# Modulation products of a two-layer diffusion step: from the mixers to VectorE in the feed-forwards

## The chip, the core and the metric

One core of a Trainium2 chip runs the whole program. It has a matrix engine (TensorE, PE in the profile), a vector engine (VectorE, DVE), an activation engine (ScalarE, ACT), GpSimd (POOL) and SyncE (SP), which issues the loads here. Each engine takes its instructions in a fixed order. The metric is the device time of one execution, in microseconds.

## What is computed

One step of a diffusion backbone: two layers with their own weights, 384 tokens (128 context, 256 latent) of width 1024, everything in float32. Cut to what matters here, a layer is

```python
mod = silu(cond) @ w_mod[l] + b_mod[l]        # nine vectors m[0..8] of 1024, for two conditions
h = x * (1 + m[1]) + m[0]
x = layer_norm(ALPHA * x + 0.5 * m[2] * swiglu(h, w_ffn_up[0], w_ffn_down[0]))
h = x * (1 + m[4]) + m[3]
x = layer_norm(ALPHA * x + m[5] * mixer(h))   # attention and a gated scan side by side
h = x * (1 + m[7]) + m[6]
x = layer_norm(ALPHA * x + 0.5 * m[8] * swiglu(h, w_ffn_up[1], w_ffn_down[1]))
```

The vectors hang on the conditions alone, `c` for latent and `c_ctx` for context tokens. So they can be worked out at any time before their use. There are eighteen, written (layer, number) below; one reads 4 MB of `w_mod`.

## The kernel before

**Stages.** The program runs feed-forward (0,0), mixer 0, feed-forward (0,1), then the same three for layer 1. Between two of them lies a boundary: a LayerNorm over the whole width, after which the next input can be made. I call the boundaries b0 to b4, and the feed-forwards the first to the fourth. In the profiled execution the first feed-forward lies at 31 to 319 us, mixer 0 at 329 to 521, the second feed-forward at 530 to 815, the third at 825 to 1102, mixer 1 at 1113 to 1306 and the fourth to 1595.

**Products.** Activations are transposed, 128 channels by 384 tokens to a chunk. A weight tile of 1 MB (`ws`, three buffers, L293) is cut in pieces; ScalarE rounds a piece to `wh` (L313), VectorE subtracts it from the original into `wl` (L314), and TensorE does three matmuls for each chunk (`mm3`, L318 to L320): high by high, high by low (`hl`), low by high. In a feed-forward's up half (22 columns f of two products each) VectorE also multiplies gate and value (L481) and makes the low part of the result (L483). In the down half it adds the product to the residual X (L349); there are 12 weight tiles, three to a pair of output chunks.

**Modulation.** The class `Pump` holds all modulation work as a list of groups, cut into steps that are taken in the list's order. Each step takes one 1 MB tile of `w_mod` (`wm`, three buffers, loaded by SP at L189). A group has one of two forms:
- the tensor form (`add_tensor`, L236): the tile goes through TensorE with the silu of the conditions as stationary operand, in four strips of 32 columns, with one or two vectors side by side. One vector takes four steps; a pair takes eight.
- the vector form (`add_vector`): half a vector, in two steps. VectorE multiplies each 128 x 512 piece by the conditions' values for the partitions and adds it up in `gsum` (L248 for the first, L250 for the others), for both conditions: 2 multiplications and 14 multiply-adds. The closing sum over the partitions (`finish`) is 8 small matmuls of `gsum` against `rows`, again at L236.

In both forms `finish` ends with a transposition (`gmt`, L228) and an addition (L229) on VectorE.

**Where steps are taken.** `PUMPED` says which vectors have which form, and in what order. `PLAN` gives, for each feed-forward, the columns of its up half and the tiles of its down half at which a step is taken; `NEXT_STEPS` the steps at each boundary (`next_input`); `MIX_STEPS` those in a mixer before its output product. So before, twelve half vectors run on VectorE beside the up halves of the first two feed-forwards, and (0,5) to (0,8), (1,0), (1,2) and (1,5) to (1,8) go through TensorE at boundaries and in the mixers.

**Order.** A scheduler orders each engine's instructions by priority as they become possible; `tc.high_priority` pulls the weight splits (by PIECE_AHEAD) and the normalisation (by CHAIN_AHEAD) ahead. Steps that are written behind a mixer's attention are therefore partly pulled forward into its products.

Of the kernel before, what the change touches and what calls it, by code (L numbers as in the profile page):

```python
# [14 lines left out]
PSUM = bass.MemoryType.PSUM  # L15

P = 128
D = 1024
KD = D // P
# [35 lines left out]
def by_vector(*mods):  # L55
    """Groups of modulation products taken by the vector engine: one vector's half each."""
    return [([x], c, c + HALF, True) for x in mods for c in (0, HALF)]


def by_tensor(*mods):  # L60
    """A group of modulation products taken by the tensor engine."""
    return [(list(mods), 0, KD, False)]


PUMPED = (by_vector((0, 2), (0, 3), (0, 4)) + by_tensor((0, 5)) + by_tensor((0, 6), (0, 7)) + by_tensor((0, 8), (1, 0))
          + by_vector((1, 1), (1, 3), (1, 4)) + by_tensor((1, 2)) + by_tensor((1, 5), (1, 6)) + by_tensor((1, 7), (1, 8)))
UP = [f for f in range(3, 21) if f % 3]
PLAN = ((UP, ()), (UP, ()), ((), ()), ((), ()))
NEXT_STEPS = (3, 3, 4, 3, 3)
MIX_STEPS = (14, 10)  # L70
# [3 lines left out]
def hybrid_step_kernel(ctx: ExitStack, tc: tile.TileContext, A):  # L74
# [91 lines left out]
    class Pump:  # L166
        """The modulation products, cut into steps that other work takes in where it suits it.

        A group has some (layer, vector) pairs and a range of their 128-wide chunks; a step takes as many
        of the contraction's chunks as fill a tile."""  # L170
# [68 lines left out]
        def add_vector(self, gi, wv, k0):  # L239
            """Sums each partition's own rows, for the ones of add_tensor to sum over the partitions."""  # L240
# [63 lines left out]
    def piece(src):  # L304
        """Exact float32 weights [P, a, b] as two float32r parts, the second what the first leaves."""
# [22 lines left out]
    def rstd_columns(ps, n, eps, name):  # L328
        """n token tiles of mean squares in ps[:, :n] -> their reciprocal roots."""
# [6 lines left out]
    class Residual:  # L336
        """Post-norm of alpha*x + gate*y, with y coming in chunk by chunk."""
# [38 lines left out]
        def moments(self):  # L376
            """Token-major mean (in PSUM) and reciprocal deviation; the mean also along the partitions."""
# [24 lines left out]
    class LastResidual(Residual):  # L402
        """Turned to token-major rows as it comes in, for the result."""
# [590 lines left out]
```

## Time and profile before

| | us |
|---|---|
| three runs | 1617.20, 1614.57, 1615.80 |
| median | 1615.8 |
| profiled execution, first to last instruction (span) | 1610.9 |
| TensorE matmuls busy | 1554.1 |
| TensorE weight loads busy | 1445.0 |
| VectorE busy | 948.3 |
| ScalarE busy | 659.3 |
| GpSimd busy | 163.0 |

The runs are of whole executions; the page doesn't give the profiled execution's own time beside its span, and the median lies 4.9 us above the span. Of the chain of waits that ends last 86% is TensorE, 5% VectorE and 2% DMA. A stretch of the trace is read by its busy columns: an engine that fills it in matmuls and in weight loads has nothing to spare, one that fills it in matmuls alone may still wait, since matmuls overlap. The granted clock is in parts of 2.4 GHz.

### The profile page before, as it was taken

To read this page: it belongs to the slowest core of one execution; us is meant where nothing else is said; L and a number is where in the kernel's file an instruction comes from. 1 tells how busy PE (TensorE), PEld (TensorE's weight loads), DVE (VectorE), ACT (ScalarE), POOL (GpSimd) and SP (SyncE) were. 2 spreads that over 40 slices of the span, in tenths; PEclk is the share of its full clock that TensorE was granted. 3 is DMA by queue.
4 is the path that set the end of the run, shared out by engine and by line. 5 is a ranking of instruction groups with operands and counts; after the bars stand their busy time and mean duration, and the time that the engine had idled before them with its cause. 6 is when DMAs were issued, how large, how long until landed. Compare 5 with 4: busy or idle time off the path is not lost.

```text
span 1610.9 us, 22640 instructions
## 1 busy us (share of the span) xinstructions
PE 1554.1 (96%) x9106; PEld 1445.0 (90%) x9106; DVE 948.3 (59%) x1556; ACT 659.3 (41%) x1066; POOL 163.0 (10%) x142
## 2 busy tenths in 40 slices
PE   6999999999999899999999999999999989999997
PEld 3899999987668899999989999997867789999996
DVE  2868764477887846873464444345788664444334
ACT  3533333258743533332353333324785444333321
POOL 0000002220004100000220000032010140000012
PEclk8999999999999999999999999999999989999998
DMA  8865653446654545663354334334465214433331
GB/s 305 272 200 175 230 169 126 117 150 207 217 191 132 178 135 182 196 215 120 125 183 134 128 122 133 124 102 164 147 191 202 73 59 131 132 130 120 129 118 40
DMA packets 210596, 249.90 MB, mean 155 GB/s; under 512 B 26298, under 2 KB 185020, under 8 KB 207420
## 3 DMA queue, kind: packets, MB, share of 16 engines
q1 hardware_dynamic: 210492, 248.47, 46.8%
q8 instruction: 71, 1.16, 0.3%
q14 instruction: 33, 0.27, 0.1%
HBM read 245.52 MB, written 1.88 MB: 154 GB/s over the span
## 4 chain that ended last, share of the span: by engine, by line
PE 86%; DVE 5%; issue 3%; DMA 2%; ACT 2%; POOL 1%; SPq 0%; DVEq 0%; POOLq 0%; ACTq 0%
PE acc L318 26%; PE acc L319 26%; PE acc L320 26%; PE gm L236 3%; DMA wm<-in_w_mod_dram 2%; PE acc L745 1%; DVE wl L314 1%; PE ms L373 1%; PE pv L778 1%; PE ms L761 0%; ACT wh L313 0%; DVE hl L284 0%; POOL sum_f L359 0%; DVE tr L866 0%; SPq L189 0%
## 5 line engine op out<-in xcount | busy, mean ns | idle before, releaser
L313 ACT CAST wh<-ws 128x1024 fp32r<-128x1024 f32 (+1 forms) x330 | 335.7, 1019 | 778.3 <-PE acc L319 552.1
L314 DVE TENSOR_TENSOR wl<-ws,wh 128x1024 fp32r<-128x1024 f32 (+1 forms) x330 | 411.1, 1247 | 389.8 <-ACT wh L313 388.7
L318 PE MATMUL acc<-hh,wh 128*128 128x384 f32 x1280 | 428.8, 339 | 7.9 <-ACT hh L276 7.4
L320 PE MATMUL acc<-hh,wl 128*128 128x384 f32 x1280 | 431.9, 338 | 2.9 <-DVE wl L314 2.9
L319 PE MATMUL acc<-hl,wh 128*128 128x384 f32 x1280 | 431.6, 338 | 1.4 <-DVE hl L284 1.4
L318 PEld LDWEIGHTS acc<-hh,wh 128*128 128x128 f32 x1280 | 242.4, 190 | 15.5 <-ACT hh L276 9.0
L320 PEld LDWEIGHTS acc<-hh,wl 128*128 128x128 f32 x1280 | 242.6, 190 | 8.6 <-DVE wl L314 5.5
L319 PEld LDWEIGHTS acc<-hl,wh 128*128 128x128 f32 x1280 | 242.4, 189 | 7.6 <-DVE hl L284 4.4
L318 PE MATMUL acc<-gh,wh 128*128 128x384 f32 x704 | 236.6, 336 | 0.0
L319 PE MATMUL acc<-gl,wh 128*128 128x384 f32 x704 | 236.1, 335 | 0.0
L320 PE MATMUL acc<-gh,wl 128*128 128x384 f32 x704 | 235.9, 335 | 0.0
L318 PEld LDWEIGHTS acc<-gh,wh 128*128 128x128 f32 x704 | 132.2, 188 | 0.4 <-issue 0.4
L319 PEld LDWEIGHTS acc<-gl,wh 128*128 128x128 f32 x704 | 132.3, 188 | 0.0
L320 PEld LDWEIGHTS acc<-gh,wl 128*128 128x128 f32 x704 | 132.2, 188 | 0.0
L481 DVE TENSOR_TENSOR a<-a,acc 128x384 f32<-128x384 f32 x88 | 48.7, 554 | 126.2 <-PE acc L320 125.7
L250 DVE SCALAR_TENSOR_TENSOR gsum<-wm,sil,gsum 128x512 f32<-128x512 f32 x168 | 120.3, 766 | 0.0
L318 PE MATMUL acc<-hh_in,wh 128*128 128x384 f32 x352 | 118.0, 339 | 2.2 <-ACT hh_in L276 2.2
L320 PE MATMUL acc<-hh_in,wl 128*128 128x384 f32 x352 | 117.8, 335 | 0.7 <-DVE wl L314 0.7
L319 PE MATMUL acc<-hl_in,wh 128*128 128x384 f32 x352 | 118.2, 336 | 0.0
L358 POOL TENSOR_TENSOR sum_f<-X 128x384 f32<-128x384 f32 x4 | 5.1, 1282 | 846.3 <-DVE X L349 846.3
L236 PE MATMUL gm<-wm,sil 128*32 128x256 f32 (+1 forms) x512 | 66.2, 532 | 13.0 <-DMA wm<-in_w_mod_dram 11.9
L318 PEld LDWEIGHTS acc<-hh_in,wh 128*128 128x128 f32 x352 | 66.2, 189 | 4.5 <-ACT hh_in L276 3.2
(260 smaller groups left out, 1721.9 us busy)
## 6 DMA issues: line engine op xcount, KB each, us to landing
ws<-in_w_ffn_up_dram SPq DMA_DIRECT2D x88, 1024.0 KB, 5.2
wm<-in_w_mod_dram SPq DMA_DIRECT2D x56, 1024.0 KB, 6.8
ws<-in_w_ffn_down_dram SPq DMA_DIRECT2D x32, 1024.0 KB, 5.0
wm<-in_w_mod_dram SPq DMA_DIRECT2D x32, 512.0 KB, 5.8
ws<-in_w_ffn_down_dram SPq DMA_DIRECT2D x16, 768.0 KB, 4.4
ws<-in_w_in_dram SPq DMA_DIRECT2D x12, 1024.0 KB, 5.4
ws<-in_w_o_dram SPq DMA_DIRECT2D x8, 1024.0 KB, 8.5
ws<-in_w_uq_dram SPq DMA_DIRECT2D x12, 192.0 KB, 3.2
```

Source lines behind the costliest of these rows:

```text
L236: nc.tensor.matmul(self.ps[32 * g : 32 * g + 32, :n], lhsT, wv[:, g], start=self.fresh, stop=stop)
L250: nc.vector.scalar_tensor_tensor(self.sum[:, r], wv[:, kk], s, self.sum[:, r], op0=ALU.mult, op1=ALU.add)
L313: nc.scalar.copy(parts[0], src)
L314: nc.vector.tensor_tensor(parts[1], src, parts[0].bitcast(F32), op=ALU.subtract)
L318: nc.tensor.matmul(ps, wh, xh, start=start, stop=False)
L319: nc.tensor.matmul(ps, wh, xl, start=False, stop=False)
L320: nc.tensor.matmul(ps, wl, xh, start=False, stop=stop)
L358: nc.gpsimd.tensor_tensor(self.sums[0], X[:, 0, :] if c == 1 else self.sums[0], X[:, c, :], op=ALU.add)
L373: nc.tensor.matmul(self.pt[:, 2 * i + j : 2 * i + j + 1], src[:, i * P : (i + 1) * P], mean_w[:, 0:1], start=False, stop=stop and i == T / ...
L481: nc.vector.tensor_tensor(a, a, px[:, :T], op=ALU.mult)
L745: nc.tensor.matmul(views[i], qT[hf][0:96, h % 4, q0 : q0 + P], kT[hf][0:96, h % 4, k0:k1], start=True, stop=True)
L778: nc.tensor.matmul(o[:, P:T], v, pTs[e][:, (j - 1) * 256 : j * 256], start=(j == 1), stop=(j == 3))
```

## The change

Five vectors change from the tensor form to the vector form: (0,6), (0,7), (1,0), (1,6) and (1,7). The others keep theirs. The places change too. The first feed-forward takes (0,2), (0,3), (0,4), (0,6) and (0,7), with steps in its down half as well; the second (1,0), (1,1) and (1,3); the third, which had none, (1,4), (1,6) and (1,7). Each boundary takes four steps, one vector in the tensor form: (0,5), (0,8), (1,2), (1,5), (1,8). The mixers take no steps; where they had them they load the next tiles, and a feed-forward without down steps does so in the middle of its down half. Comments are removed, so lines behind L55 stand one or two further down.

```diff
-PUMPED = (by_vector((0, 2), (0, 3), (0, 4)) + by_tensor((0, 5)) + by_tensor((0, 6), (0, 7)) + by_tensor((0, 8), (1, 0))
-          + by_vector((1, 1), (1, 3), (1, 4)) + by_tensor((1, 2)) + by_tensor((1, 5), (1, 6)) + by_tensor((1, 7), (1, 8)))
+PUMPED = (by_vector((0, 2), (0, 3), (0, 4), (0, 6), (0, 7)) + by_tensor((0, 5)) + by_tensor((0, 8))
+          + by_vector((1, 0), (1, 1), (1, 3)) + by_tensor((1, 2))
+          + by_vector((1, 4), (1, 6), (1, 7)) + by_tensor((1, 5)) + by_tensor((1, 8)))
 UP = [f for f in range(3, 21) if f % 3]
-PLAN = ((UP, ()), (UP, ()), ((), ()), ((), ()))
-NEXT_STEPS = (3, 3, 4, 3, 3)
-MIX_STEPS = (14, 10)
+DOWN = [j for j in range(12) if j % 3 < 2]
+PLAN = ((UP, DOWN), (UP, ()), (UP, ()), ((), ()))
+NEXT_STEPS = 4
...
-    def next_input(res, l, s, nl, nm, steps):
-        pump.step(steps)
+    def next_input(res, l, s, nl, nm):
+        pump.step(NEXT_STEPS)
         pump.finish()
...
                     if 3 * j + f0 // 8 in down_steps:
                         pump.load(WM_AHEAD)
                         pump.step()
+                    elif j == KD // 2 - 1:
+                        pump.load(WM_AHEAD)
...
-            pump.step(steps)
-            pump.finish()
-            # output product
+            pump.load(WM_AHEAD)
             res = Residual(f"m{l}", modv[l][:, 5])
```

What the order of VectorE's instructions makes of it is shown at three places. In all of them `wl` is the low part of a weight piece, without which TensorE can't go on, and `gsum` a sum of the vector form.

First place: VectorE in the down half of the first feed-forward. Before, splits and residual additions follow each other:

```order
L349 SCALAR_TENSOR_TENSOR X<-acc_2033,gate_2029,X 128x256
L314 TENSOR_TENSOR wl_2239<-ws_2208,wh_2238 128x1024
L349 SCALAR_TENSOR_TENSOR X<-acc_2034,gate_2029,X 128x128
L349 SCALAR_TENSOR_TENSOR X<-acc_2034,gate_2029,X 128x256
L314 TENSOR_TENSOR wl_2269<-ws_2266,wh_2268 128x1024
L314 TENSOR_TENSOR wl_2297<-ws_2266,wh_2296 128x1024
L314 TENSOR_TENSOR wl_2327<-ws_2324,wh_2326 128x768
L314 TENSOR_TENSOR wl_2349<-ws_2324,wh_2348 128x768
```

After, in the same part:

```order
L315 TENSOR_TENSOR wl_2324<-ws_2311,wh_2323 128x1024
L230 TENSOR_TENSOR modv_121<-gmt_2242,small_111 128x8
L249 TENSOR_SCALAR gsum_2246<-wm_0_2037,sil 128x512 x2
L251 SCALAR_TENSOR_TENSOR gsum_2246<-wm_0_2037,sil,gsum_2246 128x512 x4
L315 TENSOR_TENSOR wl_2352<-ws_2311,wh_2351 128x1024
L251 SCALAR_TENSOR_TENSOR gsum_2246<-wm_0_2037,sil,gsum_2246 128x512 x2
L251 SCALAR_TENSOR_TENSOR gsum_2246<-wm_4_2107,sil,gsum_2246 128x512 x3
L315 TENSOR_TENSOR wl_2382<-ws_2379,wh_2381 128x768
L251 SCALAR_TENSOR_TENSOR gsum_2246<-wm_4_2107,sil,gsum_2246 128x512 x5
L315 TENSOR_TENSOR wl_2404<-ws_2379,wh_2403 128x768
```

A half vector's sixteen operations stand between the last four of the six splits of one column of tiles, up to six in a row ahead of one.

Second place: VectorE in mixer 0, where the gate (`gu`, `uc`), the scan (`ti`, `tr`) and the splits of the query and key weights meet. Before:

```order
L652 SCALAR_TENSOR_TENSOR gu_3486<-gu_3486,acc_3457 128x384
L653 SCALAR_TENSOR_TENSOR uc_2877<-uc_2877,gu_3486 128x384
L854 SCALAR_TENSOR_TENSOR ti_3415<-ti_3415,uc_2879 128x384 x2
L518 COPY st_q_3440<-ms_3436 96x384
L314 TENSOR_TENSOR wl_3585<-ws_3578,wh_3584 128x512
L331 TENSOR_SCALAR v_q_3446<-ms_3442 128x3
L314 TENSOR_TENSOR wl_3628<-ws_3621,wh_3627 128x768
L638 TENSOR_TENSOR rr_2872<-tab,ms_3450 128x384
L683 COPY kT_3583<-acc_3588 64x512
L835 TENSOR_TENSOR ucl_3503<-uc_2880,uch_3502 128x384
```

After:

```order
L249 TENSOR_SCALAR gsum_5135<-wm_0_5128,sil 128x512
L230 TENSOR_TENSOR modv_121<-gmt_4695,small_111 128x16
L249 TENSOR_SCALAR gsum_5135<-wm_0_5128,sil 128x512
L251 SCALAR_TENSOR_TENSOR gsum_5135<-wm_0_5128,sil,gsum_5135 128x512 x2
L655 SCALAR_TENSOR_TENSOR gu_3631<-gu_3631,acc_3602 128x384
L856 SCALAR_TENSOR_TENSOR ti_3560<-ti_3560,uc_3024 128x384
L656 SCALAR_TENSOR_TENSOR uc_3022<-uc_3022,gu_3631 128x384
L521 COPY st_q_3585<-ms_3581 96x384
L315 TENSOR_TENSOR wl_3730<-ws_3723,wh_3729 128x512
L332 TENSOR_SCALAR v_q_3591<-ms_3587 128x3
L856 SCALAR_TENSOR_TENSOR ti_3560<-ti_3560,uc_3024 128x384
L251 SCALAR_TENSOR_TENSOR gsum_5135<-wm_0_5128,sil,gsum_5135 128x512
```

The first multiplications and three multiply-adds of (1,0) stand among them, and another comes five rows further down, ahead of the split `wl_3805`; the rest of this half, and the next half, follow in the attention and the output product.

Third place: VectorE at the start of the third feed-forward. Before, the last pieces of its input (`hl`) are followed by the first splits:

```order
L284 TENSOR_TENSOR hl_7138<-h_219_6_7205,hh_7137 128x384
L284 TENSOR_TENSOR hl_7138<-h_219_7_7213,hh_7137 128x384
L447 TENSOR_SCALAR ag_11227<-small_351 128x8
L448 TENSOR_SCALAR ag_11227<-small_351 128x8
L314 TENSOR_TENSOR wl_7330<-ws_7234,wh_7329 128x1024
L314 TENSOR_TENSOR wl_7369<-ws_7362,wh_7368 128x1024
L481 TENSOR_TENSOR a_0_7294<-a_0_7294,acc_7237 128x384
L314 TENSOR_TENSOR wl_7397<-ws_7364,wh_7396 128x1024
```

After:

```order
L249 TENSOR_SCALAR gsum_7624<-wm_0_7617,sil 128x512
L285 TENSOR_TENSOR hl_7196<-h_219_6_7263,hh_7195 128x384
L249 TENSOR_SCALAR gsum_7624<-wm_0_7617,sil 128x512
L251 SCALAR_TENSOR_TENSOR gsum_7624<-wm_0_7617,sil,gsum_7624 128x512
L285 TENSOR_TENSOR hl_7196<-h_219_7_7271,hh_7195 128x384
L251 SCALAR_TENSOR_TENSOR gsum_7624<-wm_0_7617,sil,gsum_7624 128x512 x3
L315 TENSOR_TENSOR wl_7388<-ws_7292,wh_7387 128x1024
L315 TENSOR_TENSOR wl_7427<-ws_7420,wh_7426 128x1024
L315 TENSOR_TENSOR wl_7455<-ws_7422,wh_7454 128x1024
```

Two multiplications and four multiply-adds of (1,4)'s first half stand between the last pieces of the input and the first splits.

## Rows read from the trace of the kernel before

**Rows 1.** The page's busy times: engine, busy us (share), instructions.
```profile
PE 1554.1 (96%) x9106; PEld 1445.0 (90%) x9106; DVE 948.3 (59%) x1556; ACT 659.3 (41%) x1066; POOL 163.0 (10%) x142
```
**Rows 2.** Stretches, all engines: start:end, length, busy per engine, then clock, DMA, GB/s.
```profile
825.30:1010.50 185.20, 184.69 (x1072) 183.20 (x1073) 84.93 (x113) 72.00 (x108) 6.89 (x8) 1.00 0.41 136
246.40:269.30 22.90, 22.90 (x134) 22.90 (x133) 9.11 (x10) 6.72 (x8) 2.97 (x2) 1.00 0.39 127
292.10:315.00 22.90, 22.90 (x134) 22.90 (x133) 9.16 (x10) 6.79 (x8) 6.67 (x5) 1.00 0.42 115
541.00:552.00 11.00, 9.12 (x40) 7.87 (x39) 11.00 (x18) 7.48 (x11) 2.02 (x2) 0.84 0.28 92
829.00:840.00 11.00, 11.00 (x75) 10.18 (x73) 8.30 (x21) 8.11 (x17) 4.84 (x5) 1.00 0.39 145
```
**Rows 3.** The three stretches of mixer 0 and of mixer 1, all engines.
```profile
329.40:404.00 74.60, 72.74 (x408) 61.91 (x408) 56.74 (x112) 55.57 (x99) 12.04 (x14) 0.98 0.55 175
404.00:435.00 31.00, 29.92 (x167) 24.03 (x168) 28.52 (x54) 23.20 (x37) 1.88 (x3) 1.00 0.62 213
435.00:520.70 85.70, 83.30 (x474) 62.65 (x473) 68.45 (x139) 36.64 (x86) 18.71 (x12) 1.00 0.51 170
1113.40:1189.00 75.60, 72.65 (x400) 60.90 (x400) 57.59 (x113) 55.69 (x99) 12.42 (x14) 0.98 0.55 176
1189.00:1220.00 31.00, 30.00 (x167) 24.09 (x168) 27.74 (x47) 23.29 (x37) 2.10 (x3) 1.00 0.63 216
1220.00:1306.00 86.00, 83.27 (x457) 63.94 (x455) 59.40 (x130) 36.91 (x86) 17.75 (x12) 0.96 0.27 92
```
**Rows 4.** Chain of waits, middle of mixer 0: start, us, what.
```profile
412.12 1.23 DVE wl L314
...
415.83 0.96 DVE ti L861
...
418.18 1.68 DVE tr L866 x3
```
**Rows 5.** The same six stretches, modulation products on TensorE alone (line 236).
```profile
329.40:404.00 74.60, 7.19 (x48) 1.21 (x48) 0.98 0.55 175
404.00:435.00 31.00, 4.68 (x32) 1.04 (x32) 1.00 0.62 213
435.00:520.70 85.70, 9.07 (x50) 1.54 (x50) 1.00 0.51 170
1113.40:1189.00 75.60, 6.90 (x40) 0.96 (x40) 0.98 0.55 176
1189.00:1220.00 31.00, 4.68 (x32) 1.04 (x32) 1.00 0.63 216
1220.00:1306.00 86.00, 5.92 (x32) 1.08 (x32) 0.96 0.27 92
```
**Rows 6.** Chain of waits: one closing sum, a step with two vectors, one with one.
```profile
97.89 0.57 PE gm L236 x16
...
521.06 1.00 PE gm L236 x8
...
829.22 1.00 PE gm L236 x16
```
**Rows 7.** Groups by form: VectorE's multiply-adds and multiplications; busy us, mean ns.
```profile
L250 DVE SCALAR_TENSOR_TENSOR gsum<-wm,sil,gsum 128x512 f32<-128x512 f32 x168 | 120.3, 766 | 0.0
...
L248 DVE TENSOR_SCALAR gsum<-wm,sil 128x512 f32<-128x512 f32 x24 | 11.1, 466 | 0.9 <-DMA wm<-in_w_mod_dram 0.9
```
**Rows 8.** The tile gsum: shortest, median and longest multiply-add in ns.
```profile
L250 DVE SCALAR_TENSOR_TENSOR gsum<-wm,sil,gsum x168: 724/747/1502, 60.0 to 713.5; 128x512 f32<-128x512 f32 x168
```

More of the change, by code (lines that the diff above doesn't have):

```diff
@@ L526, in token_scale, with mixer @@
         return pr
-    def mixer(l, hh, hl, steps):
+    def mixer(l, hh, hl):
         w_in = A["w_in"][l]
@@ L932, in hybrid_step_kernel @@
         res = ffn(l, 0, hh, hl, *PLAN[2 * l], first=first if l == 0 else None)
-        hh, hl = next_input(res, l, 0, l, 3, NEXT_STEPS[3 * l])
-        res = mixer(l, hh, hl, MIX_STEPS[l])
-        hh, hl = next_input(res, l, 1, l, 6, NEXT_STEPS[3 * l + 1])
+        hh, hl = next_input(res, l, 0, l, 3)
+        res = mixer(l, hh, hl)
+        hh, hl = next_input(res, l, 1, l, 6)
         res = ffn(l, 1, hh, hl, *PLAN[2 * l + 1], residual=LastResidual if last else Residual)
         if not last:
-            hh, hl = next_input(res, l, 2, l + 1, 0, NEXT_STEPS[2])
+            hh, hl = next_input(res, l, 2, l + 1, 0)
     res.finish([A["o_prompt"][0], A["o_sample"][0, :P], A["o_sample"][0, P:]])
```

## The prediction, made before the changed kernel ran

> **What bounds the kernel now.** I read the busy times first. TensorE is busy 1554.1 of 1610.9 us, and its weight loads 1445.0 [rows 1]. That says "TensorE-bound" for the whole, but the stages differ, so I next read stretches. In a feed-forward's up half without any modulation work, 825.3 to 1010.5, matmuls fill 184.69 of 185.20 us and weight loads 183.20, while VectorE has 84.93 [rows 2]. Whatever is added to TensorE there lengthens the stage by its own length. In the down half the same holds, 22.90 of 22.90, with VectorE at 9.11 to 9.16 [rows 2]. The mixers look alike in the matmul column (72.74 of 74.60, 29.92 of 31.00, 83.30 of 85.70), but weight loads fill only 61.91, 24.03 and 62.65 [rows 3]. VectorE has 28.52 of 31.00 in the middle stretch, and there the chain of waits goes through it [rows 4]: the subtraction that makes wl, then the scan's arithmetic, then TensorE.
>
> The two mixers are a ready-made test of what the modulation products cost there. Mixer 0 carries 7.19 + 4.68 + 9.07 = 20.94 us of them on TensorE (130 records) and mixer 1 6.90 + 4.68 + 5.92 = 17.50 (104 records) [rows 5], and VectorE has 153.7 us of work in the first and 144.7 in the second (sums of rows 3). Yet the three stretches add up to 191.3 us in mixer 0 and to 192.6 in mixer 1. 3.4 us less on TensorE and 9 us less on VectorE bought nothing. In the last stretch, attention and output product, 9.07 us of products stand against 5.92, and the lengths are 85.7 and 86.0; the granted clock is 1.00 with more of them and 0.96 with fewer [rows 3, 5]. There the products mostly fill time in which TensorE waits for something else, and keep its clock at the upper level (2.4 GHz).
>
> The Trainium skill, Perfetto Trace Analysis, section Identifying the Most-Contended Engine, says that matmul busy time doesn't tell how near TensorE is to its limit and that the busy share of weight loads does. By it the feed-forwards have no headroom and the mixers a quarter; the trace agrees (183.20 of 185.20 against 62.65 of 85.70). It speaks against this change, which takes work out of the stages with headroom and adds to those without.
>
> **The prices.** A step of the tensor form is 16 matmul records with one vector and 8 with two, 1.00 us on the chain either way [rows 6]; it takes four steps to a vector, 4.0 us. The busy column counts more, 17.50 us for the 13 steps (104 records of 8) in mixer 1 [rows 5], 1.35 each, since each matmul's own length is in it; I take the chain's price and keep the other as a bound. A half vector in the vector form is 2 multiplications at 466 ns and 14 multiply-adds at 766 ns on VectorE [rows 7], 11.7 us, or 11.4 at the undisturbed 747 ns [rows 8]; on TensorE its closing sum over partitions is 16 records, 0.57 us on the chain [rows 6]. Five vectors change sides, ten halves: 117 us more on VectorE, twenty steps, 20 us, less on TensorE, and 5.7 us back there in closing sums.
>
> **Part by part**, against the span of 1610.9; the measured median lies 4.9 above that, and I add the same afterwards.
>
> First feed-forward's down half: eight steps, so two thirds of the tiles carry one. TensorE gets three closing sums, 1.7 us, all on the path, since it has no idle time [rows 2]. VectorE gets a half vector per 22.9 us: 9.1 + 11.4 = 20.5. That fits, but some multiply-adds take 1502 ns, twice the median [rows 8]. I read this as GpSimd running beside them. GpSimd is busy 2.97 to 6.67 of 22.9 us here [rows 2]; if that doubles the share of multiply-adds beside it, up to 6.67 × 11.4 / 22.9 = 3.3 us come on top, 23.8 of 22.9. I take 0.5 us of slip to TensorE; bounds 0 and 4, four tiles at 0.9. Sum +2.2 (1.7 to 6). The Trainium skill, GPSIMD Engine Reference, section with the specifications, says that GpSimd's SBUF interfaces are shared with VectorE, with contention for instructions that read two SBUF inputs, as these do. By it this part costs near its upper end, 6 in place of 2.2; no row shows the two together in a down half.
>
> The boundary behind it gets a fourth step (1.00) and the last closing sum (0.57), in part in time when TensorE waits for the normalisation: +1.2 (0.6 to 3, if the fourth tile lands late and a transposition on VectorE waits for it ahead of the next hl).
>
> Mixer 0. First stretch: 48 records are one step of (0,5) and four of pairs; four of (0,8) take their place, the last of them late in the stretch. One step goes; half of it I count, since weight loads fill only 83%: −0.5 (−1.4 to +3, if the late ones meet the middle's queue). Middle stretch: four steps go, but the order puts 2 multiplications and 4 multiply-adds of (1,0) among the scan and the splits, 2 × 0.47 + 4 × 0.75 = 3.9 us on an engine with 2.5 us to spare, less some transpositions that go: +2.0 (−3 to +5). Attention and output product: six steps go and a closing sum comes, −5.4 at the most by the chain's price; VectorE gets two dozen multiply-adds instead of 14, some 8 us more on 68.45 of 85.7. One helps, the other hurts, and the comparison of the mixers says that neither did much: −0.5 (−5 to +5). Boundary behind it: three products of 1.0 us on the chain [rows 6] become one closing sum, but idle time there costs clock, as at the second feed-forward's start (0.84 in rows 2): −0.4 (−2.5 to +1.5).
>
> Second feed-forward: one closing sum fewer, −0.6. The boundary behind it is unchanged.
>
> Third feed-forward's up half: six closing sums, 6 × 0.57 = 3.4, all on the path. And its start. The second one starts with multiply-adds queued between the last hl pieces and the first wl on VectorE: in 541 to 552 TensorE is busy 9.12 of 11.00 at a clock of 0.84, while the third one, with none in its queue, has 11.00 of 11.00 at 1.00 [rows 2]. The loss is 1.88 + 11 × 0.16 = 3.6 us. After the change the same operations stand at the same place of the third one. A step of (1,2) fills 1.0 of such a wait [rows 6], so I take 2.6 (0 to 5). Together +6.0 (3.4 to 8.4). What hid these multiply-adds so far was that (1,6) and (1,7) were products in mixer 1. Its boundary: a fourth step, +0.5 (0 to 2).
>
> Mixer 1: 13 steps become the four of (1,8), with nothing added on VectorE. First stretch five to four, −0.8. Middle four to none, with VectorE's 27.74 of 31.00 as the next limit: −1.3 (−3.2 to 0). Last stretch four to none: the clock is at 0.96 there already, and mixer 0 was no longer with six; −1.2 (−5 to +1). Together −3.3 (−9 to +1).
>
> The sum: 2.2 + 1.2 − 0.5 + 2.0 − 0.5 − 0.4 − 0.6 + 6.0 + 0.5 − 3.3 = +6.6. The span would be 1617.5, the time 1622.4; I say 1622.
>
> **The rivals.** A, faster: the mixers are bound by TensorE after all, as their matmul column says. Then the steps are gained whole where VectorE leaves room: 1.0 + 5.4 + 2.0 in and behind mixer 0, 1.0 + 4.0 in mixer 1, and 3.2 in its middle, −16.6; with +2.0 in mixer 0's middle and +9.3 in the feed-forwards and at their boundaries (2.2 + 1.2 − 0.6 + 6.0 + 0.5) that is −5.3, or 1610.5. With the busy column's 1.35 for each step instead (−4.7 more, 13.4 × 0.35), and no harm at the third feed-forward's start (−2.6), it is −12.6, or 1603. I take the middle, 1607. For it speaks the matmul column of rows 3, against it that mixer 1 with fewer steps isn't shorter.
>
> B, slower: VectorE falls behind in the first down half. It decides when the multiply-adds beside GpSimd lift its load over 22.9 us for a column of tiles. The wl pieces then come late, and TensorE, which has nothing else, waits: four times 0.9 to 1.5, and the queue left over stands ahead of the normalisation; together 7 more than the forecast, 1629. For it speaks the 23.8 of the bounds above, against it that weights are loaded up to three tiles ahead and that these splits have priority.
>
> C, no change: the queue at the third feed-forward's start does no harm, because other wl pieces are ready there. The 2.6 goes, and if the middle of mixer 0 doesn't lengthen either (2.0), the sum is +2.0: 1618.
>
> That the change doesn't do what it says is out: the order shows the steps at their new places.
>
> **How the numbers follow.** A measurement of this kernel tells about 0.2% from no change, 3.2 us. The forecast's own case (1617 to 1627) gets 0.42, A 0.32, B 0.15, C 0.11. The forecast's case counts as slower in 0.31 of its 0.42 and as the same in 0.11; B is slower; C is the same in 0.07 and slower in 0.04; A is faster in 0.28 and the same in 0.04. So faster 0.28, same 0.22, slower 0.50. Cases of both signs hold most of the chance; the range reaches from A's lower end, 1603, to B's 1629 plus 2 of the bounds in mixer 0: 1603 to 1631.
>
> **What would show it.** Right: mixer 0's three stretches within 2 us of 191.3, mixer 1's at 188 to 191, the third feed-forward's up half 6 us longer, with closing sums of 0.57 in the chain and idle time on TensorE in its first ten us. The middle stretch of mixer 0 with VectorE over 29 of 31. Wrong: mixers shorter by 7 us each (A); TensorE waiting for wl in the first down half, with multiply-adds of 1.5 us (B). A clock of 0.9 or lower in the attention of both mixers would make the gains there negative and the forecast too low.

## The result, and the profile after

| | before | after |
|---|---|---|
| median of the runs, us | 1615.18 (1614.21 to 1617.20, 4 runs) | 1626.30 (1625.68 to 1627.29, 4 runs) |
| ratio to before | | 1.0059, 95% interval 1.0038 to 1.0081 |
| span of the profiled execution, us | 1610.9 | 1624.1 |

By the medians the changed kernel is slower by 11.1 us; by the ratio, 0.6%, it is 9.5 us, with an interval of 6 to 13. The direction and the range were right (1622 was said). The sizes of the parts were not: mixer 1 moved the other way, and it and b3 lie outside their bounds.

Every later run lists its time and its span, and the first is about 2.0 us above the second (1626.1 and 1624.1 for the profile of after), where the prediction added 4.9. So the profiled execution of before took about 1612.9, at the fast end of its runs, and some 2 of the 13.2 us between the two profiles are chance.

The stages, from the start of the first to the start of the last product of each in the two traces; a boundary (b) is the time between, and the down halves count from the up half's last matmul:

| stage | before | after | difference | forecast |
|---|---|---|---|---|
| first feed-forward, up | 195.65 | 195.64 | 0.0 | 0 |
| first feed-forward, down | 92.30 | 94.62 | +2.3 | +2.2 |
| b0 | 10.89 | 12.35 | +1.5 | +1.2 |
| mixer 0 | 191.28 | 194.49 | +3.2 | +1.0 |
| b1 | 8.80 | 7.40 | −1.4 | −0.4 |
| second feed-forward | 285.31 | 283.39 | −1.9 | −0.6 |
| b2 | 10.50 | 10.49 | 0.0 | 0 |
| third feed-forward | 276.65 | 282.08 | +5.4 | +6.0 |
| b3 | 11.42 | 13.80 | +2.4 | +0.5 |
| mixer 1 | 192.55 | 194.56 | +2.0 | −3.3 |
| b4 and fourth feed-forward | 289.50 | 289.58 | +0.1 | 0 |

The page's busy line, to be held beside [rows 1]:

```profile
PE 1548.4 (95%) x9202; PEld 1455.2 (90%) x9202; DVE 1048.1 (65%) x1726; ACT 659.4 (41%) x1066; POOL 161.6 (10%) x142
```

TensorE does 5.7 us less and VectorE 99.8 us more, and the span is 13.2 us longer. The six stretches of the mixers have the same ends as those of [rows 3]: 0.8 us ahead of the first product of `r_q` (L525 before, L528 after) and just behind the first attention score (L745, L748). The columns are start:end, length, then busy time of TensorE, its weight loads, VectorE, ScalarE and GpSimd, clock, DMA share, GB/s:

```profile
332.90:405.30 72.40, 70.01 (x438) 60.95 (x439) 57.77 (x120) 54.45 (x97) 11.78 (x14) 1.00 0.55 173
405.30:438.90 33.60, 29.08 (x137) 26.14 (x136) 32.08 (x53) 24.23 (x38) 1.61 (x3) 0.90 0.40 133
438.90:527.40 88.50, 82.02 (x441) 65.06 (x439) 70.65 (x149) 37.16 (x86) 16.60 (x12) 0.92 0.31 101
1124.50:1199.00 74.50, 71.01 (x441) 61.19 (x441) 57.66 (x113) 56.08 (x101) 10.40 (x14) 1.00 0.48 148
1199.00:1231.30 32.30, 26.89 (x135) 24.36 (x136) 27.76 (x47) 23.41 (x37) 1.91 (x3) 0.95 0.28 84
1231.30:1319.10 87.80, 80.62 (x425) 65.03 (x423) 58.35 (x122) 36.75 (x86) 17.76 (x12) 0.92 0.20 63
```

The modulation products on TensorE in the same stretches, which answer to [rows 5]:

```profile
332.90:405.30 72.40, 6.17 (x80) 2.12 (x80) 1.00 0.55 173
405.30:438.90 33.60, 0.00 (x0) 0.00 (x0) 0.90 0.40 133
438.90:527.40 88.50, 0.64 (x16) 0.38 (x16) 0.92 0.31 101
1124.50:1199.00 74.50, 5.96 (x80) 2.19 (x80) 1.00 0.48 148
1199.00:1231.30 32.30, 0.00 (x0) 0.00 (x0) 0.95 0.28 84
1231.30:1319.10 87.80, 0.00 (x0) 0.00 (x0) 0.92 0.20 63
```

The first stretches still hold some steps, since those of the boundary are pulled forward into them; in the middle and last stretches nothing is left but one closing sum. TensorE's matmuls are busy 82.02 of 88.50 us in mixer 0's last stretch where it was 83.30 of 85.70: less work in more time. In the middle and last stretches the clock fell from 1.00 in both to 0.90 and 0.92 in mixer 0, and from 1.00 and 0.96 to 0.95 and 0.92 in mixer 1. The attention alone, from the first score to the first output product, first mixer 0 before and after, then mixer 1:

```profile
435.00:479.30 44.30, 43.15 (x237) 25.06 (x236) 36.62 (x94) 23.22 (x65) 0.00 (x0) 1.00 0.62 210
438.90:484.60 45.70, 39.94 (x189) 26.35 (x188) 38.98 (x100) 22.34 (x60) 0.00 (x0) 0.85 0.25 80
1220.00:1263.20 43.20, 41.19 (x205) 25.29 (x204) 34.83 (x89) 22.14 (x60) 0.00 (x0) 0.92 0.31 109
1231.30:1276.40 45.10, 38.64 (x174) 26.43 (x172) 34.42 (x87) 22.05 (x60) 0.00 (x0) 0.85 0.17 53
```

The chain of waits in mixer 1 shows what the clock does (start, us, what). After, VectorE's chain in the middle from the scan's `ti` on, the first products behind it, and the first scores of the attention:

```profile
1210.81 0.96 DVE ti L863
...
1217.14 0.76 PE acc L319
1217.90 0.43 PE acc L320
1218.33 0.43 PE acc L321
...
1237.52 4.63 PE acc L748 x8
```

At the same two places before:

```profile
1200.79 0.96 DVE ti L861
...
1207.11 0.47 PE acc L318
1207.59 0.23 PE acc L319
1207.82 0.23 PE acc L320
...
1227.64 1.56 PE acc L745 x4
```

A matmul of 0.23 us takes 0.43, and a score of 0.39 us takes 0.58, until the clock is back at its upper level: the granted clock of the first 3.3 us of these products is 0.51 after and 1.00 before. VectorE's chain is as long in both (6.3 us), and 66 matmuls stand behind it up to the first score in both; they take 12.7 us before and 14.0 after. So 1.3 us of mixer 1's loss are the clock in its middle.

### The profile page after: what moved, and what is told of

It is laid out like the page before. It is cut to its first block, busy times and chain, and to the rows that moved or that the text cites. A ratio compares the mean times of both kernels' runs of the same rounds, so it can differ in the third digit from the quotient of the medians.

```text
span 1624.1 us, 23002 instructions
## 1 busy us (share of the span) xinstructions
PE 1548.4 (95%) x9202; PEld 1455.2 (90%) x9202; DVE 1048.1 (65%) x1726; ACT 659.4 (41%) x1066; POOL 161.6 (10%) x142
## 4 chain that ended last, share of the span: by engine, by line
PE 84%; DVE 7%; issue 4%; ACT 2%; POOL 1%; DMA 1%; SPq 0%; DVEq 0%; POOLq 0%; ACTq 0%
PE acc L319 25%; PE acc L320 25%; PE acc L321 25%; PE gm L237 2%; PE acc L748 2%; DVE wl L315 1%; DMA wm<-in_w_mod_dram 1%; PE ms L374 1%; DVE hl L285 1%; PE pv L781 1%; ACT wh L314 1%; PE ms L764 1%; DVE X L400 0%; DVE gsum L251 0%; POOL sum_f L360 0%
## 5 line engine op out<-in xcount | busy, mean ns | idle before, releaser
L251 DVE SCALAR_TENSOR_TENSOR gsum<-wm,sil,gsum 128x512 f32<-128x512 f32 x308 | 215.9, 752 | 0.0
L482 DVE TENSOR_TENSOR a<-a,acc 128x384 f32<-128x384 f32 x88 | 48.7, 553 | 106.7 <-PE acc L321 106.1
L320 PEld LDWEIGHTS acc<-hl_in,wh 128*128 128x128 f32 x352 | 66.5, 189 | 0.9 <-issue 0.8
```

Source lines behind the costliest of these rows:

```text
L251: nc.vector.scalar_tensor_tensor(self.sum[:, r], wv[:, kk], s, self.sum[:, r], op0=ALU.mult, op1=ALU.add)
L320: nc.tensor.matmul(ps, wh, xl, start=False, stop=False)
L482: nc.vector.tensor_tensor(a, a, px[:, :T], op=ALU.mult)
```

## The experiments

All state their time beside runs of the kernel before on the same chip; those medians lie between 1616.09 and 1617.89. Filler means matmuls on TensorE whose result isn't used. Remarks behind # in the code shown below are not in the kernels, and three dots stand for lines left out.

**e1, the base for fillers**: the steps of (0,8) and (1,8) at the start of their mixers.

```diff
     def mixer(l, hh, hl):
+        pump.step(4)
+        pump.finish()
...
     def next_input(res, l, s, nl, nm):
-        pump.step(NEXT_STEPS)
+        if s != 1:
+            pump.step(4)
```

> The changed kernel with one thing moved: the four steps of (0,8) and of (1,8) stand at the start of their mixer and not at the boundary behind it. It is the base for the next kernel. The scheduler had pulled these steps into the first stretch of the mixers anyway, so all theories expect the time of the changed kernel, 1624 to 1628, and mixers of 193 to 196 us.

Measured 1628.98 (1624.07 to 1631.94), ratio 1.0072 (1.0049 to 1.0096). Its mixers take 197.7 and 196.2 us. Time and mixers lie a little above what was expected (1628, 196); the interval still covers the changed kernel's ratio, and it serves as the base of e2 and e5.

**e2, filler between the heads**: e1 with

```diff
+            filler(tab, 1, rr[:, 0:32])          # four times among keys, queries and values
...
+                    filler(tab, 1, mx[:, 0:1].to_broadcast([P, 32]))   # behind each head's maxima
```

> The kernel before this one with idle work on TensorE in the mixers: twelve groups of four matmuls (128x32 by 128x384, result not used) per mixer, four while keys and queries are made and one behind each head's maxima, some 0.75 us each, 9 us per mixer. Nothing is added on VectorE and no load. Theory 1 (clock): the modulation steps ran in time in which TensorE waited, and without them it idles, its clock falls to the lower level and the matmuls behind each wait take twice as long. Then the filled mixers are each 1 to 4 us shorter than without, at a granted clock of 0.95 or more in middle and attention (0.85 to 0.89 in the changed kernel): 1618 to 1624. Theory 2 (VectorE): the mixers are longer because VectorE's queue carries sums of (1,0) and waits stand in another order; then the filler changes nothing, 1625 to 1629, and mixer 1, which has no such sums, stays at 194 to 195. Theory 3 (TensorE bound): the filler is added whole, 18 us, 1644.

Measured 1636.43, ratio 1.0121 (1.0106 to 1.0136): in no theory's range. The middles moved as the first says (32.3 us in both mixers at a clock of 1.00, against 34.0 and 34.7 at 0.95 and 0.90 in e1, from the first product of `r_q` to the first score), but each group between the heads waits for VectorE's maxima, and the next head's scores wait behind it in TensorE's queue. Where filler stands decides, and this run says nothing on the attention.

**e3, the products of the mixers left out** of the kernel before:

```diff
-PUMPED = (... + by_tensor((0, 5)) + by_tensor((0, 6), (0, 7)) + by_tensor((0, 8), (1, 0))
-          + by_vector((1, 1), (1, 3), (1, 4)) + by_tensor((1, 2)) + by_tensor((1, 5), (1, 6)) + by_tensor((1, 7), (1, 8)))
-NEXT_STEPS = (3, 3, 4, 3, 3)
-MIX_STEPS = (14, 10)
+PUMPED = (... + by_tensor((0, 5))
+          + by_vector((1, 1), (1, 3), (1, 4)) + by_tensor((1, 2)))
+NEXT_STEPS = (3, 0, 4, 0, 0)
+MIX_STEPS = (1, 0)
...
+    for m in modv:
+        nc.vector.memset(m, 0.0)
```

> The kernel before with the products of (0,6), (0,7), (0,8), (1,0) and (1,5) to (1,8) left out, so that those vectors are zero: the mixers and the boundaries behind them keep only the last step of (0,5). Nothing is added anywhere else, so this prices the products in the mixers by themselves. 30 steps are gone, 30 us by the chain's price. Theory 1 (clock): nothing is gained in the mixers, each is between 1 us shorter and 4 us longer, with a clock near 0.85 in the attention; the boundary behind mixer 0 is 1 to 2 us shorter; total 1612 to 1621. Theory 3 (TensorE bound): the mixers are 12 to 20 us shorter each, total 1580 to 1592. Theory 2 (VectorE's order alone): mixers of the same length or a little shorter, at any clock, 1608 to 1615.

Measured 1621.20 (10 runs), ratio 1.0029 (1.0013 to 1.0044), just above the upper edge of the first theory. Without 32 steps (the expectation counted 30) and their 32 MB of loads the kernel is not faster but 5 us slower. Mixer 0 takes 194.8 us and mixer 1 197.2, against 191.3 and 192.6. Middle and last stretch of mixer 1:

```profile
1194.00:1226.80 32.80, 27.18 (x136) 24.70 (x137) 28.57 (x47) 24.21 (x38) 1.53 (x3) 0.95 0.27 82
1226.80:1314.60 87.80, 80.62 (x425) 65.01 (x423) 58.12 (x123) 36.81 (x86) 17.76 (x12) 0.92 0.20 64
```

This rules out that TensorE bounds the mixers, and with it rival A of the prediction. For mixer 1, where VectorE has no sums in this kernel or in the changed one, it also rules these out as the cause. In mixer 0 it does not: six multiply-adds moved forward into the middle here too (3.89 us).

**e4, filler at b4 alone**, in the kernel before:

```diff
+        res.fills = (l, s) == (1, 1)
...
+                if self.fills:
+                    filler(self.tail[1], 2)                            # behind the last sums
...
+            if self.fills:
+                filler(tab, 2, rs[:, 0:1].to_broadcast([P, 32]))       # behind the deviations' broadcast
...
+                if self.fills and c == 0:
+                    filler(X[:, 0, :], 1)                              # behind the first normalised chunk
```

> The kernel before with idle work on TensorE at the boundary behind mixer 1 alone: two groups of four matmuls behind the last sums, two behind the broadcast of the deviations and one behind the first normalised chunk (result not used). In the kernel before TensorE idles there and the fourth feed-forward starts at the lower clock (0.70 in its first 11 us). Theory 1 (clock): its first 11 us run at 0.95 or more and are 2 to 3.5 us shorter, less up to 1 us by which the filler delays the broadcast: 1611 to 1614. Rival (the start is bound by ScalarE's and VectorE's pieces, whatever the clock): no gain or a loss of 1 us, 1615 to 1617.

Measured 1615.30, ratio 0.9990 (0.9974 to 1.0005): in the rival's range, and no difference as a whole. The place itself did what the first theory says. First 11 us of the fourth feed-forward with filler:

```profile
1318.20:1329.20 11.00, 11.00 (x65) 10.55 (x62) 10.10 (x22) 8.98 (x21) 6.48 (x7) 1.00 0.00 1
```

and in the kernel before:

```profile
1313.80:1324.80 11.00, 11.00 (x47) 10.55 (x48) 11.00 (x23) 8.35 (x18) 4.72 (x6) 0.74 0.00 1
```

The boundary is no longer (7.72 against 7.80 us) and the up half is 2.3 us shorter (184.98 against 187.31). e7, with the same filler there, has 184.96; in all kernels without it the up half takes 187.2 to 187.5.

**e5, filler in the waits**: e1 with the filler of e2's middle, and four groups ahead of the first scores in place of those between the heads.

```diff
             gate_branch(c)
...
+            for c in (2, 3):
+                filler(us[c], 2)
             early.close()
```

> The moved base (e1) with idle work on TensorE placed otherwise than in e2: four groups of four matmuls while keys and queries are made, and four groups behind the gate's last channels, in the wait of some 6 us ahead of the first attention scores; none between the heads, where in e2 each group made TensorE's queue wait for a head's maxima. 8 groups, some 6 us per mixer. Theory 1 (clock): the middle stretches go to 29.5 to 31 us at a clock of 1.00, the first scores run at the upper clock, and attention with output product is 2 to 3 us shorter than e1's 89.8: 1619 to 1625. Rival (waiting TensorE costs nothing, whatever its clock): filler that ends inside the waits changes nothing, 1627 to 1631, or is added in part, up to 1640.

Measured 1625.08 (1617.14 to 1627.54), ratio 1.0052 (1.0034 to 1.0070), at the upper edge of the first theory; the interval overlaps that of e1 (1.0049 to 1.0096). In the traces both mixers are shorter than in e1, by 2.9 us (194.8) and 3.7 us (192.5), with 6 us more on TensorE in each. In mixer 1 nothing else changed; in mixer 0 the scheduler also moved e1's seven multiply-adds out of the middle. Middle and last stretch of mixer 1, with the same ends as above, first e1's:

```profile
1194.50:1230.10 35.60, 30.79 (x147) 28.48 (x148) 29.50 (x50) 24.80 (x40) 1.76 (x3) 0.90 0.23 72
1230.10:1319.60 89.50, 82.51 (x423) 66.45 (x423) 58.65 (x123) 36.80 (x86) 17.75 (x12) 0.90 0.20 64
```

then e5's:

```profile
1198.50:1231.70 33.20, 31.39 (x179) 25.96 (x180) 29.28 (x50) 24.72 (x40) 2.17 (x3) 1.00 0.23 71
1231.70:1317.70 86.00, 80.96 (x456) 63.95 (x455) 58.47 (x123) 36.74 (x86) 17.75 (x12) 0.96 0.22 69
```

The middle is 2.4 us shorter and the last stretch 3.5, 2.0 of these in the attention (43.4 against 45.4, at a clock of 0.92 and 0.85). The first stretch, which has no filler, is 2.3 us longer. But e1's mixers are longer than the changed kernel's own; beside those (194.5 and 194.6) the filler gains nothing in mixer 0 and 2.0 us in mixer 1, 1.8 of them in the attention.

**e6, the five vectors left out** of the changed kernel:

```diff
-PUMPED = (by_vector((0, 2), (0, 3), (0, 4), (0, 6), (0, 7)) + by_tensor((0, 5)) + by_tensor((0, 8))
-          + by_vector((1, 0), (1, 1), (1, 3)) + by_tensor((1, 2))
-          + by_vector((1, 4), (1, 6), (1, 7)) + by_tensor((1, 5)) + by_tensor((1, 8)))
-PLAN = ((UP, DOWN), (UP, ()), (UP, ()), ((), ()))
+PUMPED = (by_vector((0, 2), (0, 3), (0, 4)) + by_tensor((0, 5)) + by_tensor((0, 8))
+          + by_vector((1, 1), (1, 3)) + by_tensor((1, 2))
+          + by_vector((1, 4)) + by_tensor((1, 5)) + by_tensor((1, 8)))
+PLAN = ((UP, ()), (UP[:8], ()), (UP[:4], ()), ((), ()))
```

> The changed kernel with the five vectors that change sides, (0,6), (0,7), (1,0), (1,6) and (1,7), left out altogether, so that they are zero; the steps at the boundaries and the other vectors stay. Against the changed kernel this takes away only what the change adds to the feed-forwards: ten half vectors on VectorE and ten closing sums on TensorE. If the closing sums are the price, each 0.57 us on the chain and 0.2 us that the next matmul takes longer, 7.7 us go: 1617 to 1621. If VectorE's load costs besides (splits that come late, queues at the boundaries), more goes, 1608 to 1616. If the mixers had gained, as rival A of the prediction has it, this kernel would be clearly faster than the one before, under 1610.

Measured 1621.84 (1616.86 to 1628.60), ratio 1.0044 (1.0025 to 1.0062), just above the first range. Against the kernel before 5.8 us stay by the medians and 7.1 by the ratio, so of the change's loss 5.3 of 11.1 us (medians) or 2.4 of 9.5 (ratios) go with what it adds to the feed-forwards, less than the 7.7 expected; the interval is 3 us wide either way. In the traces the feed-forwards and b0 together are some 7.5 us shorter than after's, near the 7.7. This kernel's matmuls are busy 18.2 us less than those of the one before and VectorE 4.8 us less, with nothing more on ScalarE and GpSimd, and it is slower.

**e7, filler at all boundaries** of the kernel before, to keep its clock up:

```diff
                 self.tail = (X[:, c, :], sq)
+                if self.name[0] == "f" and self.broadcast:
+                    filler(X[:, c, :], 3)
...
-                if self.fills and c == 0:
+                if self.fills and c == 0 or c in self.warm:            # c = 4 to 7 at b1
                     filler(X[:, c, :], 1)
```

> The kernel before with idle work on TensorE at all boundaries: three groups of four matmuls behind the last residual chunk of the first three feed-forwards, where TensorE waits some 3 us for GpSimd's sums, one group behind each of the last four normalised chunks ahead of the second feed-forward, and the five of e4 behind mixer 1. Theory 1 (clock): in some executions the clock falls at a boundary (13.6 in place of 10.3 us at the boundary behind the second feed-forward in two of six profiles); the filler keeps it up, the second and fourth feed-forwards start 2 us shorter each, and the runs scatter less: median 1607 to 1612. Rival (the clock's falls don't depend on this work, or the filler delays the LayerNorm as much): 1614 to 1620.

Measured 1626.59 (1620.44 to 1633.94), ratio 1.0068 (1.0044 to 1.0092): a miss by 15 us for the first theory and by 7 for the rival, and the scatter grew. The chain at b0 shows why:

```profile
322.14 1.07 PE ms L384 x6
323.22 4.00 PE fill L258 x24
327.21 0.73 PE ms L409 x2
327.94 3.12 PE gm L236 x48
331.06 0.64 PE ms L409 x4
```

The filler ran behind the sums, not in the wait ahead of them, at the lower clock, and the deviations' broadcast (L409) and the steps (L236) stood behind it: b0 takes 15.7 us and b3 15.8.

**e8, the change in layer 1 alone**:

```diff
-          + by_vector((1, 1), (1, 3), (1, 4)) + by_tensor((1, 2)) + by_tensor((1, 5), (1, 6)) + by_tensor((1, 7), (1, 8)))
-PLAN = ((UP, ()), (UP, ()), ((), ()), ((), ()))
-NEXT_STEPS = (3, 3, 4, 3, 3)
-MIX_STEPS = (14, 10)
+          + by_vector((1, 1), (1, 3)) + by_tensor((1, 2)) + by_vector((1, 4), (1, 6), (1, 7)) + by_tensor((1, 5)) + by_tensor((1, 8)))
+PLAN = ((UP, ()), (UP[:8], ()), (UP, ()), ((), ()))
+NEXT_STEPS = (3, 3, 4, 4, 4)
+MIX_STEPS = (14, 0)
```

> The change in layer 1 alone: (1,4), (1,6) and (1,7) in the vector form in the third feed-forward, (1,5) at its boundary, (1,8) behind mixer 1, no steps in mixer 1; layer 0 as before, with two vectors less of closing sums in the second feed-forward. From the stages of the two profiles: third feed-forward +5.3, mixer 1 +2.0, second feed-forward two closing sums fewer, -1.5, boundaries 0: 5 to 6 us more than the kernel before, 1620 to 1623. If mixer 1 was longer by chance, and gains as the prediction had it (-3.3), there is no difference, 1615 to 1618.

Measured 1619.91 (1619.53 to 1624.48), ratio 1.0032 (1.0018 to 1.0045), just under the lower edge of the first range. Mixer 1 takes 195.8 us here, mixer 0, with its steps, 192.3. Of the change's loss a third (3.8 of 11.1 us by the medians) to a half (5.2 of 9.5 by the ratios) is in layer 1.

**e9**, the steps kept in the mixers, none at b1:

```diff
-          ... + by_tensor((0, 8), (1, 0)) + by_vector((1, 1), (1, 3), (1, 4))
-PLAN = ((UP, ()), (UP, ()), ((), ()), ((), ()))
-NEXT_STEPS = (3, 3, 4, 3, 3)
-MIX_STEPS = (14, 10)
+          ... + by_tensor((0, 8)) + by_vector((1, 0), (1, 1), (1, 3), (1, 4))
+DOWN = (0, 1, 3, 4)
+PLAN = ((UP, ()), (UP, DOWN), ((), ()), ((), ()))
+NEXT_STEPS = (3, 0, 4, 3, 0)
+MIX_STEPS = (13, 13)
```

> A kernel that takes the readings so far together: the mixers keep their steps as before, and the boundary behind mixer 0 has none. (0,8) goes alone, four steps in mixer 0; (1,0) becomes a vector form in the second feed-forward, with four steps in its down half (the tiles 0, 1, 3 and 4); the 13 steps of layer 1 are all in mixer 1. By the stages: the boundary behind mixer 0 takes 7.4 in place of 8.8, as in every kernel without steps there; the second feed-forward's up half 190 to 191.5 in place of 193.0, since its input is ready without the transpositions; two closing sums more, +1.5; mixer 0 191 to 193. Theory 1: 1612 to 1615. Rival: the second feed-forward's up half was long by chance, and the closing sums make it slower, 1616 to 1619.

Measured 1618.95 (12 runs), ratio 1.0008 (0.9991 to 1.0024): no gain, and in the rival's range. b1 (7.4) and mixer 0 (191.8) came as expected, the second feed-forward's up half (191.8) nearly, and b0 and b2 were long in the profile (14.2 and 14.5 us). The rival may be right about that up half: e4 has the code of before as far as mixer 1, and its up half takes 191.5 where before's took 193.0.

**e10**, only the three steps of b1 moved into mixer 0:

```diff
-NEXT_STEPS = (3, 3, 4, 3, 3)
-MIX_STEPS = (14, 10)
+NEXT_STEPS = (3, 0, 4, 3, 0)
+MIX_STEPS = (17, 13)
```

> The kernel before with the three steps of the boundary behind mixer 0 taken inside it, ahead of the output product (17 in mixer 0 and none behind; 13 and none in layer 1). The work is the same, only the place of three steps changes. Theory 1 (the mixers have room): boundary 7.4 in place of 8.8 and second feed-forward's up half 190 to 191.5 in place of 193.0, mixer 0 no longer than 193: 1611 to 1614. Theory 3 (TensorE bound in the mixers): mixer 0 is 3 us longer, 194 to 195, and nothing is gained, 1615 to 1617.

Measured 1616.87 (12 runs), ratio 1.0001 (0.9989 to 1.0012). b1 and the second feed-forward were 1.4 and 1.2 us shorter, and mixer 0 took 4.3 us more (195.6), nearly all of it in the attention (48.7 us against 44.6, at a clock of 1.00 in both). From 14 steps to 17 the third theory holds. No count between 6 and 13 was tried, so that a mixer has room for 13 or 14 steps is shown, and that this is the best count is not.

**e11, each closing sum twice** in the changed kernel, once against zeros:

```diff
-                for r in range(2):
-                    self.add_tensor(rows[:, r], ..., r == 1)
+                for w in (0, 1):
+                    for r in range(2):
+                        self.add_tensor(zrow if w == 0 else rows[:, r], ..., w == 1 and r == 1)
```

> The changed kernel with every closing sum done twice, the first time against a column of zeros, which adds nothing to the result: 22 times 8 small matmuls more on TensorE, nothing on VectorE, no loads. If each closing sum lies on the path, as the prediction has it, each second one costs its matmuls' time, 0.43 to 0.57 us (the longer matmul behind it is paid once), in the first down half 3 x 0.5 more (95.9 to 96.4 in place of 94.6), in the third feed-forward's up half 2 to 3.5 us more: total 1634 to 1639. If they run in time that TensorE has to spare, 1626 to 1629.

Measured 1640.51, ratio 1.0137 (1.0109 to 1.0166), 1.5 above the range: 22.6 us over the kernel before where the changed one has 11.1, so 22 second sums cost about 12 us, 0.52 each. In the chain a double sum of the first down half is

```profile
255.17 1.01 PE gm L241 x32
```

in place of 0.57. The closing sums lie on the path.

## Why the prediction held, and where its steps failed

In the traces the first and third feed-forward and b0 lose 9.2 us, the mixers 5.2 and b3 2.4, while b1 and the second feed-forward gain 3.3.

**The feed-forwards' price was right, at another rate.** In the first down half TensorE stayed full. The chain of after:

```profile
249.90 0.57 PE gm L237 x16
250.47 0.37 PE acc L319
```

Besides its 0.57 us a closing sum makes the next matmul 0.20 longer (0.37 in place of 0.17). Three of them at 0.77 are the 2.3 measured; the prediction had 1.7 and a slip of 0.5 that did not come. In the third feed-forward six at 0.77 are 4.6 where the prediction had 3.4, and the queue at its start cost 0.7 and not 2.6. TensorE waited for it once, 15 us in, at a clock of 1.00:

```profile
842.19 0.38 DVE gsum L251
...
843.10 1.22 DVE wl L315
...
844.37 0.45 PE acc L321
```

The 3.6 us lost at the start of the second feed-forward, from which the 2.6 was taken, are thus not the price of these multiply-adds alone; that stretch (541 to 552) also begins 11.5 us into its feed-forward and the one it was held against (829 to 840) 3.7. The two errors cancel, 5.4 against 6.0, which is luck. Of rival C the first half came nearly true; the second did not, since mixer 0's middle lengthened.

**Rival B did not come.** VectorE had room in the down half, and the chain there has no wait for it:

```profile
246.00:270.00 24.00, 24.00 (x152) 23.55 (x151) 20.03 (x28) 6.73 (x8) 2.97 (x2) 1.00 0.59 203
270.00:294.00 24.00, 24.00 (x152) 23.55 (x151) 20.85 (x28) 6.77 (x9) 5.92 (x4) 1.00 0.63 215
```

It is busy 20.03 and 20.85 of 24.00 us, the forecast's 20.5 without the 3.3 for GpSimd. Of the 56 multiply-adds there the median took 742 ns, and only one, of 1500 ns, ran beside a GpSimd instruction:

```profile
L251 DVE SCALAR_TENSOR_TENSOR gsum<-wm,sil,gsum x56: 735/742/1500, 229.6 to 312.4; 128x512 f32<-128x512 f32 x56
```

The Trainium skill's rule on the shared interfaces (GPSIMD Engine Reference, section Specifications) isn't contradicted by this, since GpSimd was busy 2.97 and 5.92 us of these two columns; but the 6 us that the prediction worked out from it for this part did not come, 2.3 did.

**The step that failed is the mixers' sum.** The prediction saw that the products there fill waits and keep the clock up, and yet took 0.5 off mixer 0's first and its last stretch and 3.3 off mixer 1. Its bounds let mixer 1 lose 1 us at the most; it lost 2.0. By stretch, in us, divided at the first product of `r_q` and at the first score:

| | mixer 0, forecast | measured | mixer 1, forecast | measured |
|---|---|---|---|---|
| first | −0.5 | −2.2 | −0.8 | −1.1 |
| middle | +2.0 | +2.7 | −1.3 | +1.3 |
| attention and output product | −0.5 | +2.7 | −1.2 | +1.8 |

The first stretches gained, and mixer 0's middle came near the forecast, with VectorE at 32.08 of 33.60 us. What failed are both last stretches and mixer 1's middle. Of mixer 0's last 2.7 us, 1.4 lie in the attention and 1.3 behind its first output product, where the clock was 1.00 in both kernels; what made these 1.3 is open.

Each trace is one execution, but nearly all of them agree on the sign:

| | without steps in middle and last stretch | with 13 or 14 steps |
|---|---|---|
| mixer 0, us | 194.5, 197.7, 194.8, 195.3, 197.2 (after, e1, e3, e6, e11) | 191.3, 192.2, 192.3, 191.8 (before, e4, e8, e9) |
| mixer 1, us | 194.6, 196.2, 197.2, 195.1, 195.8, 196.0 (after, e1, e3, e6, e8, e11) | 192.6, 191.6, 192.9, 192.9 (before, e4, e9, e10) |

e7 stands apart: its mixers have the steps and take 193.0 and 197.7; its mixer 1 begins behind the slowed boundary. Taking the steps away costs about 3 us in each mixer.

How far the clock is the cause can be told for mixer 1. Its middle lost 1.3 us in the same 66 matmuls, behind an equally long chain of VectorE. Its attention goes with its clock more than with its work: it takes 41.0 us at 1.00 (e4), 42.1 and 42.2 at 0.96 (e9, e10), 43.4 at 0.92, be it with products (before) or with e5's filler, 43.1 at 0.88 with neither (e6, e8), and 45.2 to 45.4 at 0.85 (after, e1, e3, e11). Two fall out: e2, whose filler waits there, and e7, 46.5 at 0.89. In e5 filler on TensorE alone raised that clock and shortened the attention by 1.8 to 2.0 us, with no change to the loads or to VectorE's work. So "with TensorE idle its clock falls, and the stretch behind the wait is longer than what was saved" is shown for mixer 1's middle and, by these runs, well supported for its attention. For mixer 0 it is argued: e5 gained nothing there beside after, and without the steps six or seven multiply-adds stand in VectorE's queue in the middle (after, e1, e3, e6, e11) where before has none, so that queue remains a rival.

The prediction's last sentence on what would prove it wrong named this case: a clock of 0.9 or lower in the attention of both mixers. It was 0.85 in both, as the rows above show. It could have been the forecast: the trace of before already had 0.96 in the mixer with fewer steps.

The rule on weight loads (the Trainium skill, Perfetto Trace Analysis, section Identifying the Most-Contended Engine), which spoke against the change, agrees with e3: stages whose weight loads filled three quarters or little more gave nothing back when work was taken out.

**b3 was probably chance.** In after it took 13.8 us and in before 11.4, beyond the bound of +2. But b2, which has the same steps in after, e1 and e3, takes either 10.5 or 13.8 us. After's b2 and b3, from the end of the last product:

```profile
818.40:828.60 10.20, 8.45 (x85) 6.03 (x83) 6.58 (x15) 2.65 (x6) 1.70 (x2) 1.00 0.61 208
1110.90:1124.50 13.60, 11.92 (x85) 7.58 (x84) 6.67 (x16) 2.69 (x6) 1.79 (x2) 0.75 0.60 198
```

e3's b2:

```profile
816.50:830.10 13.60, 11.80 (x86) 7.86 (x84) 6.68 (x16) 2.70 (x6) 1.76 (x2) 0.75 0.53 170
```

and e1's b3, the same code as after's:

```profile
1113.10:1123.40 10.30, 8.61 (x85) 6.04 (x83) 6.67 (x16) 2.70 (x6) 1.77 (x2) 1.00 0.68 216
```

Where such a boundary is long, the clock is 0.75. In the chain of after's b3 the sums (L384) take 1.49 us and the four steps 4.75:

```profile
1114.68 1.49 PE ms L384 x2
...
1117.24 4.75 PE gm L237 x46
```

In e1's they take about half:

```profile
1116.84 0.75 PE ms L384 x2
...
1118.15 2.72 PE gm L237 x46
```

In both TensorE had waited some 3 us for GpSimd's sums, and the work behind runs at either level of the clock. With the b3 of 10.5 that e1, e2, e5, e6, e8 and e11 have, the fourth step there costs nothing, and the two profiles differ by 9.9 us. After itself has one trace only, so that its b3 is long in every execution is not ruled out.

**What moved the right way for another reason:** b1 and the second feed-forward gave 3.3 us where the prediction had 1.0. Without steps b1 takes 7.4 us in every kernel but e11 (8.0, with a double closing sum), against 8.8, and the clock lost there (0.96) did not eat the gain. Of the 1.9 us of the second feed-forward 1.6 can be chance: before's up half took 193.0 us, with a clock of 0.85 in its first 11.5 us, and e4's, with the same code and a clock of 1.00 there, 191.5.

The point forecast of 1622 stands 4 below the result, and its span of 1617.5 stands 6.6 below the 1624.1 measured. It priced the mixers at −2.3 where they cost +5.2, and b3 at +0.5 where it took +2.4; b1 and the second feed-forward made 2.3 of this good. The rest of the nearness is luck: the 4.9 us added from span to time are 2.0 in the runs.

No kernel was found that clearly beats the one before; e4's filler behind mixer 1 is worth 2.3 us at its place, which the scatter of the whole hides.

## What to carry to other kernels

Work that runs in an engine's waits can be free, and in this kernel's mixers it was worth more than free on TensorE, where it went with a higher clock for what came behind; it became a cost between 14 and 17 steps a mixer. Moving such work to another engine pays only if what is left of it adds nothing to a stage that is full: here each half vector on VectorE left a closing sum of 0.77 us on TensorE, in stages without idle time. A full matmul column doesn't say that TensorE is the bound; compare two stages with different amounts of the work, or leave the work out once.

## What had not been expected of the hardware

A boundary with the same code takes 10.2 to 10.3 or 13.6 us in different kernels' profiles, by the clock (1.00 or 0.75). The runs of one kernel scatter by 4 us either way (1612.16 to 1619.95 in 19 runs of the kernel before), and the mean clock goes with it: 0.986 at 1612.40, 0.981 at 1618.95. And leaving out 32 steps of work and 32 MB of loads made this kernel 0.3% slower.
